# Encoder trunk in seven-product blocks: the up parts' two groups staggered, and the first weight sums issued at other places

## The chip, the cores and the metric

One core of a Trainium2 chip runs the program. The metric is the device time of one execution in microseconds (us). Short names: PE is TensorE (matmuls; PEld its weight loads), DVE is VectorE, ACT is ScalarE, POOL is GpSimd, SP is SyncE, which here only issues transfers.

## The reference

One layer of an encoder on 512 tokens of 1024 channels. The end of the layer is what matters here:

```python
x = x + token_mixer(rmsnorm(x, norm_mix), ...)
x = x + cross_attention(rmsnorm(x, norm_xattn), rmsnorm(mem, norm_mem), w_xq, w_xkv, w_xo)
x = x + squared_relu_mlp(rmsnorm(x, norm_mlp), w_up, w_down)
return rmsnorm(x, norm_final)

def squared_relu_mlp(xn, w_up, w_down):          # w_up 1024 x 4096, w_down 4096 x 1024
    return jnp.square(jax.nn.relu(xn @ w_up)) @ w_down
```

## The kernel before

The trunk function goes through the token mixer, the cross attention, and then three kinds of parts that this study is about: the **output part** (the attention's output times `w_xo`), and, four times, an **up part** and a **down part** of the MLP, each pair for 1024 of the 4096 hidden columns. The parts are numbered `st`: -1 is the output part, 0, 2, 4, 6 are up parts, 1, 3, 5, 7 down parts.

**Seven products.** Each part is a product of matrices that are cut in two by two blocks and multiplied with seven block products instead of eight. They are called P1 to P7. Each is done for two **groups** `g` (0 and 1, written a and b, so 3a is P3 of the first group); a group is half of the columns (up) or half of the inner dimension (down). A part so has 14 **jobs** (P, g). Every fp32 operand is split into a high and a low part (`split_out`, L258: ACT copies the high part, DVE subtracts it from the source), and a product is three matmuls (high x high, high x low, low x high). A job of an up part is 24 matmuls of 256 columns (L1471 to L1473), a job of a down part 12 of 512 columns (`product`, L1214 to L1216).

**Order of the jobs.** PE runs in the order that the program writes (`manual_schedule`). On ACT, DVE, POOL and SP the framework orders the instructions: of those that are ready, it takes the one that stands first in the program; what is inside `tc.high_priority()` comes before the rest. `MORDER` (L1127) lists the jobs of up parts (entry 0: 1a 2a 1b 2b 5a 5b 3a 3b 6a 6b 7a 7b 4a 4b) and of down parts (entry 1: 1a 1b 5a 5b 2a 2b 6a 6b 3a 3b 7a 7b 4a 4b, with 4a and 4b run together). `JOBS` (L1076) is the order of the output part: P1 P7 P2 P5 P6 P3 P4, each a then b.

**Weights.** P1, P2 and P3 take a block of the weights as it is; SP loads it into one of three `st` buffers (`mload`). The other four take sums of blocks, which POOL's transfers form: a first transfer writes a block into a buffer, further ones add blocks to it in the memory (`mfill` with `accumulate`, L1142). Two sums run per group. The *chain* begins as block (0,1) plus (0,0), which P5 uses; after P5's split (1,1) is added for P6, after P6's split (1,0) for P4. The *pair* is (0,1) plus (1,1), for P7. There are two buffers, `msum`: the one that holds the chain of a part holds the pair of the part before (`pair_buf` is `chain_buf(st + 1)`). So the next part's chain can begin when this part's P7 is split, and the next part's pair when this part's P4 is split. `sum_start(st, pair)` (L1150) issues the first two transfers of both groups; `msplit` (L1165) calls it after the splits of 7b and 4b, and splits the weights of each job into `wh` and `wl`. There are three buffers of each, so the split of a job begins when the job two places ahead of it begins (`mahead`, L1185).

For the first up part `sum_start` is called for chain and pair at job 8 of the output part (L1232), with all its transfers tied behind the last add of `w_xo` (`behind`, L1157). POOL also computes the power -1/2 of the norm, once for each half of the tokens (`rstd_half`, L1351); PE spreads the result over the partitions (`norm_half`, L1369), and from there come the MLP's activations `xf`.

**Banks and activations.** In an up part P1, P6, P7 and P4 of a group add up in one PSUM bank, P5 and P3 in a second one, and P2 has a third. Between two of them the bank is read: ACT copies P1 (L1477), P5 (L1484) and P6 (L1487), DVE subtracts P7 from a kept copy (L1492) and P2 adds with L1479. After the square of the ReLU (L1446, L1447) the results are combined into the seven **forms** that the down part takes as its left operand; `form` splits each into high and low. The forms for P1, P2 and P4 are made as soon as their product is read. Those for P5 (L1499), P3 and P6 (L1502, L1503) and P7 (L1507) need P4's result and are made, for both groups, after the last job of the up part. In a down part (`by_blocks`) P1, P6, P7 and P4 share two banks, P5 and P3 two, P2 has two; each finished product is added to the residual `xr` by DVE (`add_to`, L1418), and the next user of the bank waits for that.

## Time and profile before

| what | value |
|---|---|
| median of 3 runs | 871.79 us (869.49 to 872.32) |
| the profiled execution's own time | 872.12 us |
| its span, first to last instruction | 870.3 us |
| mean granted PE clock | 0.972 |
| busy: PE, DVE, ACT, POOL | 823.4, 624.8, 482.5, 116.8 us |
| transfers in the span | 131.53 MB, mean 151 GB/s |
| first up part to last down part | 508.35 to 863.0 us |

Durations that are quoted later come from the one profiled execution, so sums are made against its own time; it lies 1.8 us above its span and 0.3 us above the median of the runs.

How to read the rows: a timeline row has start and length in us, the engine, the line, the operation, what it writes and reads, its shape, how many instructions were merged, and in brackets the idle time of the engine just ahead of it with what ended it. A group row ends in the busy time, the mean length of one in ns, and the idle time ahead. A waits row has the total, how often, and the longest. A window row has the stretch, its length, the busy time and count of the engine that was asked for, the granted PE clock as a share of the full one, the busy share of the 16 DMA engines and their GB/s. A row of the chain that ended last has start, length and what it was.

### The profile page before, as it was taken

What the parts mean: (1) busy time and instruction counts of PE and PEld (TensorE: products, weight loads), DVE (VectorE), ACT (ScalarE), POOL (GpSimd) and SP (SyncE); (2) the same over time, 40 slices, a digit from 0 to 9 for tenths busy, and PEclk for the clock granted to TensorE, in tenths of its full rate; (3) what the DMA queues carried; (4) which work ended last, traced back from release to release, by engine and by line L of the source; (5) the groups of instructions that cost most, each with busy time, mean ns of one, the idle gap of its engine ahead of it and who ended that gap; (6) DMA issues with size and microseconds to landing.
All of it is one profiled execution on the core that took longest, in us unless ns stands there. A gap on an engine that the chain in (4) does not pass through costs nothing.

```text
span 870.3 us, 13082 instructions
## 1 busy us (share of the span) xinstructions
PE 823.4 (95%) x4990; PEld 708.7 (81%) x4990; DVE 624.8 (72%) x1033; ACT 482.5 (55%) x850; POOL 116.8 (13%) x164
## 2 busy tenths in 40 slices
PE   9999999999999999999999689979997999799976
PEld 6788888888889888878888579968996899589955
DVE  6568875898589896555679469966596659655876
ACT  5247455435685674554466457834683468336834
POOL 2000000000100001000001212203221322032301
PEclk9999999999999999999999979989998999799989
DMA  7332223132333345423523948979997999789962
GB/s 275 100 128 97 74 73 121 61 99 73 121 98 122 103 141 169 116 79 102 140 61 86 260 102 169 239 174 231 226 236 178 238 223 227 178 213 233 241 142 96
DMA packets 44752, 131.53 MB, mean 151 GB/s; under 512 B 4305, under 2 KB 4433, under 8 KB 44690
## 3 DMA queue, kind: packets, MB, share of 16 engines
q0 software_dynamic: 19648, 56.63, 31.7%
q1 hardware_dynamic: 24752, 73.60, 24.8%
q8 instruction: 39, 0.64, 0.3%
q10 hardware_dynamic: 290, 0.47, 0.2%
q14 instruction: 23, 0.19, 0.1%
HBM read 128.58 MB, written 2.10 MB: 150 GB/s over the span
## 4 chain that ended last, share of the span: by engine, by line
PE 61%; issue 14%; DMA 12%; DVE 6%; ACT 5%; POOL 2%; POOLq 0%; ACTq 0%; DVEq 0%
DMA as<-in_wpk 10%; PE mm L261 10%; PE mm L263 10%; PE mm L262 10%; PE sm L1214 4%; PE sm L1215 3%; PE sm L1216 3%; ACT wh L258 3%; PE mm L1472 3%; DVE wl L258 3%; PE mm L1473 3%; PE mm L1471 3%; PE sm L485 2%; PE sm L1471 2%; PE sm L1472 2%
## 5 line engine op out<-in xcount | busy, mean ns | idle before, releaser
L258 ACT ACTIVATE wh<-st 128x1024 fp32r<-128x1024 f32 x123 | 129.9, 1058 | 155.1 <-PE mm L262 43.7
L258 DVE TENSOR_TENSOR wl<-st,wh 128x1024 fp32r<-128x1024 f32 x123 | 150.2, 1223 | 83.1 <-ACT wh L258 82.2
L1142 POOL DMA_DIRECT2D as<-in_wpk x96 | 87.0, 968 | 261.4 <-DVE wl L258 166.8
L258 DVE TENSOR_TENSOR wl<-as,wh 128x1024 fp32r<-128x1024 f32 x66 | 80.8, 1224 | 52.3 <-ACT wh L258 52.0
L261 PE MATMUL mm<-xT,wh 128*128 128x512 f32 x288 | 115.4, 402 | 0.0
L263 PE MATMUL mm<-xT,wl 128*128 128x512 f32 x288 | 113.4, 394 | 0.1
L262 PE MATMUL mm<-xT,wh 128*128 128x512 f32 x288 | 112.7, 391 | 0.3 <-DVE xT L975 0.3
L258 ACT ACTIVATE wh<-as 128x1024 fp32r<-128x1024 f32 x66 | 69.7, 1056 | 77.2 <-DMA as<-in_wpk 25.1
L1214 PE MATMUL sm<-wh,a 128*128 128x512 f32 x180 | 75.1, 417 | 22.2 <-DVE vv L1418 22.2
L1216 PE MATMUL sm<-wh,a 128*128 128x512 f32 x180 | 73.7, 409 | 0.7 <-DVE a L258 0.7
L1215 PE MATMUL sm<-wl,a 128*128 128x512 f32 x180 | 73.7, 409 | 0.0
L263 PEld LDWEIGHTS mm<-xT,wl 128*128 128x128 f32 x288 | 54.1, 188 | 11.7 <-DVE wl L258 0.3
L261 PEld LDWEIGHTS mm<-xT,wh 128*128 128x128 f32 x288 | 54.2, 188 | 11.1 <-ACT wh L258 0.3
L262 PEld LDWEIGHTS mm<-xT,wh 128*128 128x128 f32 x288 | 54.2, 188 | 11.0 <-DVE xT L975 0.9
L1214 PEld LDWEIGHTS sm<-wh,a 128*128 128x128 f32 x180 | 36.2, 201 | 33.0 <-issue 20.8
L1216 PEld LDWEIGHTS sm<-wh,a 128*128 128x128 f32 x180 | 36.0, 200 | 9.1 <-DVE a L258 1.0
L1215 PEld LDWEIGHTS sm<-wl,a 128*128 128x128 f32 x180 | 36.3, 201 | 7.6
L1472 PE MATMUL sm<-xT,wh 128*128 128x256 f32 x128 | 36.7, 286 | 1.0 <-DVE xT L258 1.0
L1471 PE MATMUL sm<-xT,wh 128*128 128x256 f32 x128 | 36.9, 288 | 0.6 <-ACT xT L258 0.6
L199 POOL TENSOR_TENSOR tiny<-tiny,misc 128x4 f32<-128x4 f32 (+1 forms) x10 | 9.6, 965 | 204.6 <-DVE tiny L197 139.5
L1473 PE MATMUL sm<-xT,wl 128*128 128x256 f32 x128 | 36.6, 286 | 0.0
L1471 PE MATMUL mm<-xT,wh 128*128 128x256 f32 x128 | 36.3, 284 | 0.0
(387 smaller groups left out, 2135.5 us busy)
## 6 DMA issues: line engine op xcount, KB each, us to landing
st<-in_wpk SPq DMA_DIRECT2D x123, 512.0 KB, 3.7
as<-in_wpk POOLq DMA_DIRECT2D x100, 512.0 KB, 7.5
gate<-in_wpk POOLq DMA_DIRECT2D x8, 512.0 KB, 5.8
as<-in_x SPq DMA_DIRECT2D x4, 512.0 KB, 6.7
vv<-in_x SPq DMA_DIRECT2D x8, 256.0 KB, 4.1
out<-vv SPq DMA_DIRECT2D x7, 256.0 KB, 2.2
a<-in_mem SPq DMA_DIRECT2D x2, 512.0 KB, 3.7
t<-in_rows SPq DMA_DIRECT2D x2, 256.0 KB, 4.9
```

Of the source, the lines that this page charges most:

```text
L258: return sc.activation(dst_hi, src, AF.Copy), v.tensor_tensor(out=dst_lo, in0=src, in1=dst_hi.bitcast(F32), op=ALU.subtract)
L261: pe.matmul(ps, lhsT=ah, rhs=bh, start=first, stop=False)
L262: pe.matmul(ps, lhsT=ah, rhs=bl, start=False, stop=False)
L263: pe.matmul(ps, lhsT=al, rhs=bh, start=False, stop=last)
L485: mm = pe.matmul(ps[64 * i:64 * i + 64, z:z + 64], lhsT=kc[j][:, w * P + 64 * i:w * P + 64 * i + 64], rhs=rhs(j, w * P, i), start=True, st ...
L1142: return eng.dma_start(out=dst, in_=mblock(st, g, *b), **kw)
L1214: pe.matmul(ps, lhsT=ah, rhs=bh, start=new, stop=False, **fl)
L1215: pe.matmul(ps, lhsT=ah, rhs=bl, start=False, stop=False, **fl)
L1216: pe.matmul(ps, lhsT=al, rhs=bh, start=False, stop=end and k == 1, **fl)
L1471: pe.matmul(o, lhsT=hi[:, z], rhs=xh[:, m], start=new, stop=False, **fl)
L1472: pe.matmul(o, lhsT=hi[:, z], rhs=xl[:, m], start=False, stop=False, **fl)
L1473: pe.matmul(o, lhsT=lo[:, z], rhs=xh[:, m], start=False, stop=kt == 3, **fl)
```

## The change

Up parts get orders of jobs of their own. The first one: 1a 2a 1b 2b 5a 5b 3a 6a 3b 7a 6b 4a 7b 4b. The other three: 1a 2a 5a 3a 5b 1b 6a 2b 7a 6b 4a 3b 7b 4b. Down parts keep theirs. `sum_start` takes the groups that it is for, and `msplit` now calls it for each group by itself, after that group's P7 and P4.

The four late forms are made per group: those of the first group inside the up part, right after job 4a; of the second group the P5 form after 4b, and the P6, P3 and P7 forms by a function `ready`, which the down part calls ahead of its jobs 5a, 2a and 6a.

For the first up part the chain sums are issued at job 5 of the output part, tied to nothing; the pair sums are issued in `rstd_half` of the second half, tied behind its power.

```diff
             if p == "P6":
-                last_xo[0] = add_block(s_, block(-1, g, 1, 0))
+                add_block(s_, block(-1, g, 1, 0))
...
-    MORDER = ([("P1", 0), ("P2", 0), ("P1", 1), ("P2", 1)] + two("P5", "P3", "P6", "P7", "P4"), two("P1", "P5", "P2", "P6", "P3", "P7", "P4"))
-    MJ = [(st, p, g) for st in range(8) for p, g in MORDER[st % 2]]
+    seq = lambda s: [("P" + w[0], "ab".index(w[1])) for w in s.split()]
+    MORDER = [seq("1a 2a 1b 2b 5a 5b 3a 6a 3b 7a 6b 4a 7b 4b")] + [two("P1", "P5", "P2", "P6", "P3", "P7", "P4"),
+              seq("1a 2a 5a 3a 5b 1b 6a 2b 7a 6b 4a 3b 7b 4b")] * 4
+    MJ = [(st, p, g) for st in range(8) for p, g in MORDER[st]]
...
-    def sum_start(st, pair):
+    def sum_start(st, pair, gs, after=None):
...
-                for g in range(2):
+                for g in gs:
                     o = mfill(gp, (pair_buf if pair else chain_buf)(st, g), st, g, b, i > 0)
-                    if st == 0:
-                        behind(o, last_xo[0])
+                    if after is not None:
+                        behind(o, after)
...
-            if g == 1 and p in ("P7", "P4"):
-                sum_start(st + 1, p == "P4")
+            if p in ("P7", "P4"):
+                sum_start(st + 1, p == "P4", (g,))
...
-            if n == 8:
+            if n == 5:
                 msum.extend([A16(), A16()])
-                sum_start(0, False)
-                sum_start(0, True)
+                sum_start(0, False, (0, 1))
...
         for a in adds:
             behind(a, pw)
+        if u == 1:
+            sum_start(0, True, (0, 1), pw)
...
+        def first(g):
+            v.tensor_tensor(out=y[3, g], in0=y[2, g], in1=y[3, g], op=ALU.subtract)
+            form("P5", g, y[3, g], A4)
+
+        def second(g):
+            v.tensor_tensor(out=y[3, g], in0=y[3, g], in1=y[0, g], op=ALU.subtract)
+            form("P6", g, y[3, g], A4)
+
+        def third(g):
+            v.tensor_tensor(out=y[1, g], in0=y[1, g], in1=y[3, g], op=ALU.add)
+            form("P3", g, y[1, g], A4)
+
+        def fourth(g):
+            v.tensor_tensor(out=y[0, g], in0=y[0, g], in1=y[2, g], op=ALU.subtract)
+            form("P7", g, y[0, g], A4)
...
             elif p == "P4":
                 y[2, g] = T2()[:, 0:512]
                 square(y[2, g], ps)
-        for g in range(2):
-            v.tensor_tensor(out=y[3, g], in0=y[2, g], in1=y[3, g], op=ALU.subtract)
-            form("P5", g, y[3, g], A4)
-        for g in range(2):
-            v.tensor_tensor(out=y[3, g], in0=y[3, g], in1=y[0, g], op=ALU.subtract)
-            v.tensor_tensor(out=y[1, g], in0=y[1, g], in1=y[3, g], op=ALU.add)
-            form("P3", g, y[1, g], A4)
-        for g in range(2):
-            form("P6", g, y[3, g], A4)
-            v.tensor_tensor(out=y[0, g], in0=y[0, g], in1=y[2, g], op=ALU.subtract)
-            form("P7", g, y[0, g], A4)
+                first(g)
+                if g == 0:
+                    second(g)
+                    third(g)
+                    fourth(g)
...
+        def ready(p, g):
+            for at, fn in ((("P5", 0), second), (("P2", 0), third), (("P6", 0), fourth)):
+                if (p, g) == at:
+                    fn(1)
+                    hand(1)
...
-        by_blocks(2 * f + 1, sta, (sm2, mm2, sm2), lambda t, c, ps, sign, last: add_to(t, c, ps, sign, f == 3 and last))
+        by_blocks(2 * f + 1, sta, (sm2, mm2, sm2), lambda t, c, ps, sign, last: add_to(t, c, ps, sign, f == 3 and last), ready)
```

In the new text the P2 form of a group is made when both its P3 and its P6 are done; `hand` gives the down part the forms that exist so far.

## Prediction

> **What bounds the kernel now.** I read the page first, then the busy time by stretches, cut where TensorE's lines change from up products (L1471 to L1473) to down products (L1214 to L1216), then TensorE's waits, then the timelines around the two places that they name.

> ```profile
> PE 823.4 (95%) x4990; PEld 708.7 (81%) x4990; DVE 624.8 (72%) x1033; ACT 482.5 (55%) x850; POOL 116.8 (13%) x164
> 508.35:554.64 46.29, 43.25 (x345) 0.96 0.71 163
> 554.64:601.36 46.72, 41.57 (x171) 0.93 0.83 196
> 601.36:641.67 40.31, 40.31 (x337) 1.00 0.99 240
> 641.67:688.05 46.38, 41.19 (x171) 0.93 0.84 201
> 688.05:728.36 40.31, 40.31 (x338) 1.00 0.99 237
> 728.36:776.41 48.05, 41.57 (x170) 0.89 0.80 195
> 776.41:816.73 40.32, 40.32 (x338) 1.00 1.00 238
> 816.73:863.00 46.27, 40.17 (x170) 0.93 0.60 149
> PE sm L1214 <- DVE vv L1418: 22.2, 7, 6.1
> PE sm L1369 <- POOL tiny L1351: 9.9, 1, 9.9
> ```

> TensorE (PE) is busy for 95%, so only its holes are to be had. The eight stretches are up and down in turn; the columns are length, PE busy, granted clock, DMA share and GB/s. The last three up parts take 40.31 us without a hole and at clock 1.00: 14 jobs of 2.88 us. The down parts take 46.27 to 48.05 us and lose clock. The waits say where: 22.2 us in the down parts, and 9.9 us once, ahead of L1369.

> That one first: POOL's timeline ahead of it, PE's row, and the clock in that stretch.

> ```profile
> 477.50 2.51 POOL L1142 DMA_DIRECT2D as<-in_wpk  x3
> 500.41 1.18 POOL L1142 DMA_DIRECT2D as<-in_wpk  x1 [8.22 <-DMA as<-in_wpk]
> 501.16 1.17 POOL L1351 TENSOR_TENSOR tiny<-tiny,misc 128x2 f32<-128x2 f32 x1
> 502.38 0.69 PE L1369 MATMUL sm<-cs,tiny 128*128 128x128 f32 x2 [9.88 <-POOL tiny L1351]
> 497.74:507.98 10.24, 5.60 (x14) 0.50 0.65 122
> ```

> The power that the first half's norm needs (L1351) stands on POOL behind the eight transfers of the first up sums; the last accumulate waits 8.22 us for the transfer it adds to. PE stands for 9.88 us, and the clock falls to 0.50.

> Now the first down part: the DMA on the chain of waits, then ACT, DVE and PE; below them the first matmuls of jobs 1 and 5.

> ```profile
> 560.69 11.54 DMA as<-in_wpk
> 568.77 1.06 ACT L258 ACTIVATE wh<-as 128x1024 fp32r<-128x1024 f32 x1 [4.67 <-DMA as<-in_wpk]
> 566.80 0.67 DVE L1418 TENSOR_TENSOR vv<-vv,sm 128x512 f32<-128x512 f32 x1
> 569.87 1.23 DVE L258 TENSOR_TENSOR wl<-as,wh 128x1024 fp32r<-128x1024 f32 x1 [2.39 <-ACT wh L258]
> 576.90 1.87 DVE L1418 TENSOR_TENSOR vv<-vv,sm 128x512 f32<-128x512 f32 x3
> 577.64 0.80 PE L1214 MATMUL sm<-wh,a 128*128 128x512 f32 x1 [4.08 <-DVE vv L1418]
> 576.25:583.07 6.82, 5.43 (x13) 0.50 0.69 154
> 554.64 0.40 PE L1214 MATMUL sm<-wh,yT 128*128 128x512 f32 x1
> 565.55 0.39 PE L1214 MATMUL mm<-wh,gate 128*128 128x512 f32 x1
> 647.46 11.78 DMA as<-in_wpk
> 735.75 11.45 DMA as<-in_wpk
> 822.82 12.74 DMA as<-in_wpk
> ```

> Four jobs take 10.91 us, 2.73 each, so a down part without holes is 14 x 2.73 = 38.2 us. P6 adds to the banks of P1, so PE has to wait until DVE has read P1 out (L1418). One such read runs at 566.80; the next stand behind the split of P6's weights, which waits for a sum that lands 11.54 us after its issue, and behind forms of the activations. They run at 576.90, though P1 was over by 560. PE loses 4.08 us, and 6.8 us at half clock. The last three rows are the same transfer on the chain in the other down parts. So a down part is bounded by late sums and by DVE's order, not by the amount of work.

> **The change part by part.** *First sums.* The chain sums move to job 5 of the output part, whose P5 weights free the buffer; the pair sums move behind the second power.

> ```profile
> 514.19 0.70 POOL L1351 TENSOR_TENSOR tiny<-tiny,misc 128x2 f32<-128x2 f32 x1 [11.87 <-DVE tiny L1349]
> DMA to landing us min/median/max: 3.2/7.3/12.7
> 508.35:555.00 46.65, 41.45 (x50) 0.96 0.71 165
> 531.63 0.39 PE L1472 MATMUL mm<-yT,wh 128*128 128x256 f32 x1 [1.00 <-DVE yT L258]
> ```

> The first power then finds POOL free, and the 9.88 us go. At half clock 5.60 us of matmuls cost 2.8 us more than at full, so at most 12.7 us are gained. But DVE, busy for 41.45 of the 46.65 us that follow, is late next: PE already waits 1.00 us for P3's activations at 531.63. I take 11.0; the ends are 8.9 (one more wait of 1.0) and 12.7. The chain sums pass the two adds of P6 on POOL and share the DMA engines with SP's loads; they go out three jobs of 2.73, some 8 us, before today's 477.50, so two medians of 7.3 us in a row end by 485, ahead of the power, which is ready when PE goes idle at 492.5. [...] The new wait: the pair sums stand behind the second power, about 503 instead of 514.19. Two chained medians bring them to 518; P7 of the first group is job 9, due near 529 (554.64 less 11.0 and five jobs of 2.88) and split two jobs earlier at 523. Nothing, with 5 us to spare; beyond that each us late is a us on PE. Behind the power stand only the P5 adds.

> *Down parts.* Today both groups' P7 and P4 follow each other, so the next part's sums bunch. POOL's sum transfers by stretches (busy, count, clock, DMA share, GB/s):

> ```profile
> 521.00:540.00 19.00, 4.76 (x4) 1.00 0.72 141
> 540.00:562.00 22.00, 7.39 (x10) 1.00 0.99 250
> ```

> Ten are issued in 22 us at DMA share 0.99, four in the 19 us before. With the groups staggered, P7 and P4 of the first group split as jobs 8 and 10 instead of 10 and 12, so that group's four transfers go two jobs (5.8 us) earlier and are done as the down part begins. In front of P5's adds then stands one pair accumulate instead of two. I estimate that the adds land about 3 us sooner after their issue: 8.5 instead of 11.54. The second add today lands at 572.2; P6's second group would be due at 554.64 + 7 x 2.73 = 573.8 and its split takes 2.3 us, so it was late by only about a us. Also, the second group's P6, P3 and P7 forms are now put out inside the down part, after P1's reads in the program, so these reads no longer queue behind them. What is late next is the read of P7's bank before P4, for which I leave 0.4 us a part. The four parts take 187.4 us; 4 x 38.6 is 154.4: 33.0 saved. The ends are 34.6 (nothing left) and 0 (below). A loss I exclude for the DMA side: the transfers are the same in number and start no later, but for the second group's chain sums, one job later and needed only at job 3. SP's loads spread out from the first four jobs to jobs 0, 1, 3, 5: nothing.

> *Up parts: two waits that the change adds.* In the last three up parts 3a follows 5a at once and adds to the bank that ACT must first copy; in all four 4b follows 7b at once, on a bank that DVE must first subtract. Today a job lies between them. Timelines of ACT and DVE, and groups of DVE:

> ```profile
> 615.83 1.06 ACT L258 ACTIVATE wh<-st 128x1024 fp32r<-128x1024 f32 x1
> 616.80 0.58 ACT L1484 ACTIVATE t<-mm 128x512 f32<-128x512 f32 x1
> 636.11 0.69 DVE L1492 TENSOR_TENSOR t<-t,sm 128x512 f32<-128x512 f32 x1 [0.43 <-PE sm L1473]
> L258 DVE TENSOR_TENSOR a<-t,a 128x512 fp32r<-128x512 f32 x24 | 16.5, 686 | 1.4 <-ACT a L258 1.4
> L1502 DVE TENSOR_TENSOR t<-t,as 128x512 f32<-128x512 f32 x8 | 5.5, 684 | 0.0
> L258 DVE TENSOR_TENSOR wl<-as,wh 128x1024 fp32r<-128x1024 f32 x64 | 78.4, 1224 | 52.0 <-ACT wh L258 51.7
> ```

> For 3a: at the end of 5a ACT starts a weight split at 615.83, and the copy is over at 617.38, so PE waits 1.6 us (0.8 if the copy goes first, 2.6 with a second split ahead). While 3a waits, the following jobs' split has gone on; nothing else queues on PE but the later jobs. For 4b: the subtract takes 0.69 us and can begin with the end of 7b: 1.0 us at best. But four forms of the first group stand ahead of it in the program, eight DVE pieces of 0.69, or 5.5 us. They can begin about 2.1 us after 4a, behind a split and two squares on ACT; of the 5.8 us until the end of 7b some 3.7 are left, and two splits of 1.22 and a subtract of 0.68 take 3.1 of these. If all that goes first, with one more piece for P2's form, the subtract ends 5.9 us after 7b. The row at 636.11 speaks for the short end, the reads that waited until 576.90 behind program-earlier forms for the long one; between rows of equal weight I take the middle, 3.4 us. In the first up part 7b follows 4a directly, so the forms aren't ready yet: 1.3 us (1.0 to 2.0).

> *The sum,* against the profiled execution, 872.12 us with a span of 870.3: -11.0 + 1.3 + 3 x (1.6 + 3.4) - 33.0 = -27.7, so a span of 842.6 and a time of 844.4. The median of the runs shown, 871.79, is 0.3 below that execution: 844.

> [...] The idle stretches that here went with half clock were 4.08 us and more, and the 1.00 us one did not. [...] The trace has no idle stretch between the two sizes. [...]

> **The rivals.** *The new wait at 4b is the long one.* All forms of the first group go ahead of the subtract: 5.9 us instead of 3.4, long enough for the half clock, which in 576.25:583.07 cost half of 5.43, 2.7 us. 3 x (2.5 + 2.7) = 15.6 more: 860. For it speaks that the order on DVE follows the program among what is ready; against it that DVE has holes while it waits for ACT (52.0 us in the row of the splits).
> *The down parts keep their holes.* The adds of P5 still wait in POOL's line behind a pair accumulate and the DMA engines, 0.99 busy in the up parts, stay full. It decides where the second add takes over some 10.6 us to land instead of 11.54. Then the 33.0 us aren't saved while the new waits stay: 877, slower by 5. Against it: the DMA share falls to 0.83 in the down part, and one accumulate less is ahead.
> *The change doesn't free the power.* Nothing ties the chain accumulates to a place ahead of the first power but their earlier readiness; if they wait there again, 9.9 us come back: 854.

> **How the numbers follow.** The forecast 844 has 0.54, the long wait 0.32, the holes that stay 0.06, the power that stays behind 0.08. The low end takes the good ends: -12.7 + 1.0 + 3 x (0.8 + 1.0) - 34.6 = -40.9, which is 831. The high end is the first rival with 1.0 more at each 3a: 863. That leaves out the second rival and the tails. About 0.3%, 2.6 us, is what a measurement of this kernel can tell from no change. All but the second rival are faster by more: 0.92; slower 0.06; the rest, where the ends of two cases cancel, 0.02.

> **What would show it.** Right: no wait of L1369 on POOL beyond a us or two; down parts of 38 to 39 us at clock 1.00; the waits of L1214 on L1418 under 2 us in all; up parts of 45 us with a wait of L1471 on ACT L1484 near 1.6 and on DVE L1492 near 3.4. Wrong: up parts near 50 us with half clock at their end (first rival), down parts still over 45 us with a DMA of 11 us on the chain (second), or the 9.9 us still ahead of L1369 (third).

## The result: slower by 0.8%

| | median | ratio to before, 95% interval |
|---|---|---|
| before | 871.79 us (869.49 to 874.07, 7 runs) | |
| after | 878.85 us (875.74 to 882.65, 7 runs) | 1.0082 [1.0055, 1.011] |

The forecast was 844 us with a range of 831 to 863. The profiled execution of the changed kernel took 878.85 us with a span of 877.1. Of the four executions of `e12_no_handout`, one of the kernels below, one took 2069.5 us against 863.94 to 866.19 for the others, and no time below counts it.

This is the same cut by parts as before, TensorE alone (length, busy time and matmul rows, granted clock, DMA share, GB/s); the first row is the first up part.

```profile
496.09:549.10 53.01, 47.08 (x345) 0.90 0.74 183
549.10:599.04 49.94, 41.75 (x170) 0.90 0.78 182
599.04:650.14 51.10, 42.92 (x337) 0.93 0.94 232
650.14:688.91 38.77, 38.39 (x171) 1.00 0.81 183
688.91:741.36 52.45, 43.32 (x338) 0.91 0.94 232
741.36:780.48 39.12, 38.74 (x170) 0.99 0.76 174
780.48:831.28 50.80, 42.72 (x337) 0.93 0.95 232
831.28:869.74 38.46, 38.46 (x170) 1.00 0.52 121
```

| part | before | after | change | forecast of the change |
|---|---|---|---|---|
| start of the first up part | 508.35 | 496.09 | -12.3 | -11.0 |
| first up part | 46.29 | 53.01 | +6.7 | +1.3 |
| first down part | 46.72 | 49.94 | +3.2 | -8.1 |
| three later up parts | 120.94 | 154.35 | +33.4 | +15.0 |
| three later down parts | 140.70 | 116.35 | -24.4 | -24.9 |

The first and the last row came as forecast, within 1.3 us. Three went wrong, all to the long side: the later up parts by 18.4 us, the first down part by 11.3, the first up part by 5.4. TensorE's waits (total, how often, the longest) name three places:

```profile
PE sm L1490 <- ACT a L258: 20.3, 3, 7.1
PE mm L1490 <- ACT t L1503: 6.8, 4, 2.1
PE sm L1216 <- ACT a L258: 6.8, 1, 6.8
PE sm L1216 <- DVE vv L1421: 1.1, 3, 0.4
```

The first row is 4b in the later up parts, the second 3a in all four, the third 5b in the first down part. The last row was 22.2 us before the change.

**The power.** POOL's timeline shows the power (now L1352) run as soon as its input is there; its matmul (now L1372) follows on TensorE at 492.69 without a wait:

```profile
491.92 0.71 POOL L1352 TENSOR_TENSOR tiny<-tiny,misc 128x2 f32<-128x2 f32 x1 [13.82 <-DVE tiny L1350]
```

**4b.** VectorE's queue around the end of 7b in the second up part (the dots stand for rows left out), then TensorE's row for 4b. 7b ended 6.67 us ahead of 645.07, at 638.40.

```profile
636.43 0.69 DVE L1458 TENSOR_TENSOR t<-t,t 128x512 f32<-128x512 f32 x1
637.04 0.68 DVE L1509 TENSOR_TENSOR rg<-mm,rg 128x512 f32<-128x512 f32 x1
637.64 1.21 DVE L258 TENSOR_TENSOR wl<-st,wh 128x1024 fp32r<-128x1024 f32 x1
638.77 0.68 DVE L258 TENSOR_TENSOR a<-t,a 128x512 fp32r<-128x512 f32 x1
639.49 0.69 DVE L1462 TENSOR_TENSOR t<-t,as 128x512 f32<-128x512 f32 x1
...
643.64 0.68 DVE L1470 TENSOR_TENSOR as<-as,t 128x512 f32<-128x512 f32 x1
644.24 0.68 DVE L1513 TENSOR_TENSOR t<-t,sm 128x512 f32<-128x512 f32 x1
645.07 0.55 PE L1490 MATMUL sm<-xT,wh 128*128 128x256 f32 x1 [6.67 <-ACT a L258]
```

The stretch of half clock around it, all engines (PE, PEld, DVE, ACT, POOL, then clock and transfers):

```profile
643.06:649.89 6.83, 4.82 (x22) 4.85 (x23) 3.24 (x6) 2.49 (x4) 1.30 (x2) 0.50 0.92 232
```

VectorE has no hole in this stretch. L1458, L1462, L1466 and L1470 and the low halves behind them are the four forms of the first group; 7b's subtract (L1513), which 4b waits for, comes last. The row names ScalarE as the releaser, but that form is of the first group and only happened to end at 644.99; the subtract, which 4b needs, ended at 644.92, 0.15 us ahead of 4b. In the stretch of half clock 4.82 us of matmuls ran at 0.50, which costs 2.4. So this part is 40.31 + 1.52 at 3a + 6.67 at 4b + 2.4 = 50.9, measured 51.10.

**5b in the first down part.** The timelines of ScalarE, VectorE and TensorE:

```profile
551.80 0.63 ACT L1450 ACTIVATE t<-t 128x512 f32<-128x512 f32 x1
558.24 1.06 ACT L258 ACTIVATE wh<-as 128x1024 fp32r<-128x1024 f32 x1 [5.81 <-DMA as<-in_wpk]
563.53 0.63 ACT L258 ACTIVATE a<-t 128x512 fp32r<-128x512 f32 x1 [1.30 <-DVE t L1458]
559.33 1.23 DVE L258 TENSOR_TENSOR wl<-as,wh 128x1024 fp32r<-128x1024 f32 x1 [5.92 <-ACT wh L258]
562.81 0.68 DVE L1458 TENSOR_TENSOR t<-t,t 128x512 f32<-128x512 f32 x1
564.21 0.79 PE L1216 MATMUL sm<-wh,a 128*128 128x512 f32 x1 [6.76 <-ACT a L258]
```

And the transfer on the chain of work that ended last:

```profile
546.60 11.56 DMA as<-in_wpk
```

The second group's sum for 5b is issued at 546.60 and lands 11.56 us later. The split of those weights heads the queues of ScalarE and VectorE meanwhile, and the square of 4b was over at 552.4; yet L1458, the first step of 5b's form, runs at 562.81, behind the split. So the late sum cost more than its own lateness; `e12b_no_handout` below shows how much more.

**3a in the first up part.** There 5b lies between 5a and 3a, and the forecast had no wait. ScalarE and TensorE:

```profile
520.05 1.06 ACT L258 ACTIVATE wh<-as 128x1024 fp32r<-128x1024 f32 x1 [4.24 <-DMA as<-in_wpk]
...
521.96 0.58 ACT L1503 ACTIVATE t<-mm 128x512 f32<-128x512 f32 x1
522.59 0.38 PE L1490 MATMUL mm<-yT,wh 128*128 128x256 f32 x1 [2.05 <-ACT t L1503]
```

The new order has 6a right behind 3a, so the split of 6a's weights comes up two jobs ahead of that, while its sum is still under way; the copy of 5a's result stands behind it on ScalarE. Right behind the wait, 523.60 to 527.01 ran at half clock, with TensorE busy throughout, which costs another 1.7 us.

### The profile page after: what moved, and what is told of

Its sections match the earlier page's. It is cut to its first block, busy times and chain, and to the rows that moved or that the text cites. A ratio compares the mean times of both kernels' runs of the same rounds, so it can differ in the third digit from the quotient of the medians.

```text
span 877.1 us, 13066 instructions
## 1 busy us (share of the span) xinstructions
PE 824.6 (94%) x4990; PEld 711.7 (81%) x4990; DVE 624.6 (71%) x1033; ACT 484.2 (55%) x850; POOL 117.1 (13%) x164
## 4 chain that ended last, share of the span: by engine, by line
PE 57%; DMA 14%; issue 10%; DVE 9%; ACT 6%; POOL 2%; POOLq 0%; ACTq 0%; DVEq 0%
DMA as<-in_wpk 12%; PE mm L261 11%; PE mm L263 11%; PE mm L262 10%; DVE wl L258 3%; PE sm L1218 3%; PE sm L1216 3%; PE sm L1217 3%; ACT wh L258 3%; PE sm L485 2%; POOL as L1144 2%; DMA gate<-in_wpk 2%; PE sm L827 1%; PE mm L1216 1%; PE mm L1218 1%
## 5 line engine op out<-in xcount | busy, mean ns | idle before, releaser
L258 DVE TENSOR_TENSOR wl<-st,wh 128x1024 fp32r<-128x1024 f32 x123 | 150.1, 1222 | 71.5 <-ACT wh L258 70.8
L258 ACT ACTIVATE wh<-st 128x1024 fp32r<-128x1024 f32 x123 | 129.6, 1057 | 127.8 <-PE mm L262 43.7
L258 DVE TENSOR_TENSOR wl<-as,wh 128x1024 fp32r<-128x1024 f32 x66 | 80.8, 1224 | 76.2 <-ACT wh L258 75.3
L258 ACT ACTIVATE wh<-as 128x1024 fp32r<-128x1024 f32 x66 | 69.9, 1059 | 106.7 <-DMA as<-in_wpk 29.9
L1216 PE MATMUL sm<-wh,a 128*128 128x512 f32 x180 | 71.6, 398 | 7.9 <-ACT a L258 6.8
L1218 PE MATMUL sm<-wh,a 128*128 128x512 f32 x180 | 71.2, 396 | 1.1 <-DVE a L258 1.1
L1217 PE MATMUL sm<-wl,a 128*128 128x512 f32 x180 | 71.0, 395 | 0.0
L1490 PE MATMUL sm<-xT,wh 128*128 128x256 f32 x128 | 40.8, 319 | 21.8 <-ACT a L258 20.3
L1216 PEld LDWEIGHTS sm<-wh,a 128*128 128x128 f32 x180 | 34.3, 191 | 16.7 <-ACT a L258 7.2
L1490 PEld LDWEIGHTS sm<-xT,wh 128*128 128x128 f32 x128 | 28.3, 221 | 23.0 <-ACT a L258 20.9
L1491 PE MATMUL sm<-xT,wh 128*128 128x256 f32 x128 | 40.1, 314 | 1.7 <-DVE xT L258 1.7
L1218 PEld LDWEIGHTS sm<-wh,a 128*128 128x128 f32 x180 | 34.3, 191 | 9.0 <-DVE a L258 1.8
L1217 PEld LDWEIGHTS sm<-wl,a 128*128 128x128 f32 x180 | 34.4, 191 | 7.1
L1492 PE MATMUL sm<-xT,wl 128*128 128x256 f32 x128 | 39.8, 311 | 0.0
```

The costliest lines, as they stand in the source:

```text
L258: return sc.activation(dst_hi, src, AF.Copy), v.tensor_tensor(out=dst_lo, in0=src, in1=dst_hi.bitcast(F32), op=ALU.subtract)
L1216: pe.matmul(ps, lhsT=ah, rhs=bh, start=new, stop=False, **fl)
L1217: pe.matmul(ps, lhsT=ah, rhs=bl, start=False, stop=False, **fl)
L1218: pe.matmul(ps, lhsT=al, rhs=bh, start=False, stop=end and k == 1, **fl)
L1490: pe.matmul(o, lhsT=hi[:, z], rhs=xh[:, m], start=new, stop=False, **fl)
L1491: pe.matmul(o, lhsT=hi[:, z], rhs=xl[:, m], start=False, stop=False, **fl)
```

## The experiments

The theory: each of the three losses is one instruction that stands in its engine's queue behind something that need not go first. The main rival: the stagger, or the waits of 4b and 5b, cost that much whatever the order on ScalarE and VectorE. Ratios are to the kernel before in the same series (medians there 872.4 to 875.1 us). "Sums" is the moved first sums, "handing out" the forms made between the down products.

| kernel | sums | handing out | stagger | median | ratio, 95% interval |
|---|---|---|---|---|---|
| e5_sums_only | yes | | | 860.48 | 0.9871 [0.9822, 0.9919] |
| e3_handout_only | | yes | | 861.37 | 0.9866 [0.9828, 0.9905] |
| e2_orders_back | yes | yes | | 848.00 | 0.9709 [0.967, 0.9749] |
| e12_no_handout | yes | | yes | 865.93 | 0.989 [0.9867, 0.9913] |
| after | yes | yes | yes | 878.85 | 1.0082 [1.0055, 1.011] |

### One instruction moved: the subtract behind 7b

```diff
-                v.tensor_tensor(out=y[3, g], in0=y[3, g], in1=ps, op=ALU.subtract)
+                with tc.high_priority():
+                    v.tensor_tensor(out=y[3, g], in0=y[3, g], in1=ps, op=ALU.subtract)
```

> The changed kernel with one instruction moved in VectorE's queue: the subtract behind 7b is written with high priority, so that it stands behind the second form's subtract and ahead of five of the first group's other pieces. Jobs, orders, sums and forms are as changed. Theory (4b waits for the subtract, and the subtract for its place in VectorE's queue): 4b's wait in the last three up parts falls from 6.6 to 7.1 us to 2.5 to 3.5 us, each such part from 51 us to about 47 us, or 44 us where the half clock at its end goes too; time 862 to 869 us. Rival (4b waits for its weights or for ScalarE, the subtract's place only goes along with that): the gap and the time stay, 876 to 881 us.

868.19 us, ratio 0.9954 [0.9927, 0.9981]. VectorE and TensorE at the same place (L1514 is the subtract), and the cut of the second up part:

```profile
637.22 0.69 DVE L1462 TENSOR_TENSOR t<-t,as 128x512 f32<-128x512 f32 x1
637.83 0.68 DVE L1514 TENSOR_TENSOR t<-t,sm 128x512 f32<-128x512 f32 x1
638.66 0.36 PE L1490 MATMUL sm<-xT,wh 128*128 128x256 f32 x1 [2.27 <-DVE t L1514]
```

```profile
597.02:641.61 44.59, 40.80 (x338) 1.00 0.94 238
```

The subtract now stands behind L1462, and 4b waits 2.27, 2.98 and 2.69 us in the three parts; they take 44.59, 48.60 and 46.49 us. The rival falls: the place in VectorE's queue alone was worth about 4 us a part, and more where the half clock went with it.

### The three pieces of the change apart

e2 puts back the orders, e3 puts the sums back too:

```diff
-    MORDER = [seq("1a 2a 1b 2b 5a 5b 3a 6a 3b 7a 6b 4a 7b 4b")] + [two("P1", "P5", "P2", "P6", "P3", "P7", "P4"),
-              seq("1a 2a 5a 3a 5b 1b 6a 2b 7a 6b 4a 3b 7b 4b")] * 4
+    MORDER = [[("P1", 0), ("P2", 0), ("P1", 1), ("P2", 1)] + two("P5", "P3", "P6", "P7", "P4"),
+              two("P1", "P5", "P2", "P6", "P3", "P7", "P4")] * 4
```

> The changed kernel with both orders of the up parts put back (the two groups side by side); the forms are still handed out between the down products and the first sums issued in mid-output. Theory (the stagger alone costs the last three up parts their 10.5 to 12.1 us; the handing out alone gives the down parts their 7.6 to 8.9 us): last three up parts 40.3 us each, last three down parts 38.5 to 39.5 us, the output part 12 us shorter, the first up part 47 to 50 us; about 832 us, and up to 845 us if the first down part still waits at 5b. Rival (the down parts became short because the staggered up part finishes the first group early, so the handing out needs the stagger): down parts 44 to 46 us, 855 to 862 us.

> The handing out of the forms alone: orders of the up parts and places of the first sums as before the change. Theory (the three parts of the change add up): the four down parts 38.5 to 40 us instead of 46 to 48 us, all else as before, 840 to 846 us. Rival (the handing out needs the stagger): 866 to 873 us.

> The kernel before with the first weight sums alone issued at the changed kernel's places; orders and forms as before. Theory (the freed power shortens the output part by 12 us, and the first up part gives 2 to 4 us of it back at its start, where its first products wait for the normalised input): first up part starts at 496 us and takes 48 to 50 us instead of 46.3 us; time 861 to 864 us. Rival (the 5.4 us that the first up part lost beyond the forecast all come from the moved sums, which land later for it): first up part 52 to 53 us, time 866 to 868 us.

e5 came in just below its range (860.48), and its first up part, 48.50 us, is the theory's. e2's cut, the second up part and the second down part:

```profile
589.75:630.81 41.06, 40.81 (x337) 1.00 1.00 232
630.81:672.47 41.66, 38.93 (x170) 1.00 0.91 223
```

TensorE at 5b of the second down part:

```profile
642.24 0.50 PE L1218 MATMUL sm<-wh,a 128*128 128x512 f32 x1 [2.16 <-DVE a L258]
```

The up parts are short again, 40.3 to 41.1 us, as the theory has it. The down parts are not 38.5 to 39.5 us but 41.7, 41.9 and 44.8, since 5b now waits 2.16 us for the low half of its form (4b, which the form needs, is the job just ahead of the down part). In the last one 5b waits 1.03 us more and half clock comes in. So e2 missed its 832 us by 16 (by 3 the 845 us that it gave for a wait at 5b in the first down part, which was 2.52 us), and e3 its 840 to 846 us by 15; neither came into its rival's range. What I took for the handing out's gain in the later down parts was the stagger's in part. The sums and the handing out do add up: 12.1 and 11.2 us below 872.53, together 24.5.

The fourth corner is the stagger without handing out: the late forms are all written behind the up part.

```diff
                 square(y[2, g], ps)
-                first(g)
-                if g == 0:
-                    second(g)
-                    third(g)
-                    fourth(g)
+        for fn in (first, second, third, fourth):
+            for g in range(2):
+                fn(g)
```

> The changed kernel, staggered and with its sums in mid-output, but with no form handed out: all the groups' last forms are written behind the up part again. Theory (stagger and handing out conflict: the forms handed out stand ahead of 7b's subtract in VectorE's queue): 4b waits at most 3 us in the last three up parts, which take 42 to 45 us instead of 51 us; the down parts get part of their holes back, 41 to 46 us instead of 38.8 us; 865 to 877 us. Rival (the stagger makes 4b late by itself, whatever stands in the queue): up parts stay at 50 to 52 us and the down parts grow, over 885 us.

Its 865.93 us are in the theory's range. A second run of the same kernel gave the trace:

> The staggered kernel without the handing out once more, for its trace. It was timed at 865.9 us where the changed kernel has 878.9 us. Theory (stagger and handing out conflict in VectorE's queue): the last three up parts 42 to 45 us, 4b waiting at most 3 us, and the down parts 41 to 46 us. Rival (the gain over the changed kernel lies in the first up and down parts, and 4b still waits 6 us and more later on): the last three up parts 48 us or more, with the first up and down parts together under 95 us.

865.22 us, span 863.4. The second pair of parts, then TensorE at 4b in it:

```profile
593.64:641.29 47.65, 42.54 (x338) 0.96 0.92 234
641.29:680.30 39.01, 38.59 (x170) 1.00 0.84 193
```

```profile
636.85 0.36 PE L1490 MATMUL sm<-xT,wh 128*128 128x256 f32 x1 [3.12 <-DVE t L1513]
```

Here both expectations missed in part. 4b waits 3.12 to 3.22 us, just over the theory's 3, and the up parts are 47.6 to 48.5 us, 3 above it. But the down parts, 39.0 to 40.2 us, are about as short as after the change, 38.5 to 39.1: with the first group finished early, what it has ready fills VectorE's holes without being handed out (in the second up part its first form, L1458, runs at 632.10, ahead of 7b's subtract at 636.02).

This trace also parts the two costs at 5b in the first down part. VectorE and ScalarE there:

```profile
551.74 0.68 DVE L1458 TENSOR_TENSOR t<-t,t 128x512 f32<-128x512 f32 x1
557.71 1.06 ACT L258 ACTIVATE wh<-as 128x1024 fp32r<-128x1024 f32 x1 [6.46 <-DMA as<-in_wpk]
```

The sum is nearly as late as after the change (the split starts at 557.71 instead of 558.24), but L1458 of the second group stands ahead of the split, and 5b waits 2.11 us instead of 6.76. So some 2 us are the sum's lateness, and the other 4.6 the form's place behind the split, where the handing out had put it.

By lengths, in us:

| | sums only | + handing out | + stagger | all three |
|---|---|---|---|---|
| first up and down part | 96.94 | 93.75 | 97.35 | 102.95 |
| three later up parts | 120.93 | 122.49 | 143.74 | 154.35 |
| three later down parts | 143.24 | 128.34 | 118.61 | 116.35 |

The stagger alone gives 24.6 us in the later down parts and takes 22.8 in the up parts: a wash. The handing out on top of it adds 10.6 us to the up parts and 5.6 to the first pair, and takes 2.3 off the later down parts. Without the stagger it is worth 16.5 us by these lengths. They are of single executions, and the one of "sums only" took 866.17 us, 5.7 above that kernel's median; by the medians the handing out is worth 12.5 us there. The ratios say the same: the stagger takes 0.987 to 0.989, within the noise, the handing out 0.987 to 0.971 without the stagger and 0.989 to 1.008 with it. Both pieces shorten the later down parts, and each is in the other's way.

### The first down part: where 7b stands

```diff
-    MORDER = [seq("1a 2a 1b 2b 5a 5b 3a 6a 3b 7a 6b 4a 7b 4b")] + ...
+    MORDER = [seq("1a 2a 1b 2b 5a 5b 3a 6a 3b 7a 6b 7b 4a 4b")] + ...
```

> The changed kernel with 7b one place earlier in the first up part (6b 7b 4a 4b at its end instead of 6b 4a 7b 4b); nothing else. Theory (the first down part's 5b stood 6.8 us because the second group's weight sum is sent only after 7b's weights are split and behind the first group's pair sum, and the form of 5b is queued behind that split): 5b's wait 2 to 4 us, the first down part 45 to 47 us instead of 49.9 us, time 873 to 876 us. Rival (5b waits for its form, which is late because the up part ends on 4b; the sum is not what ends last): wait 6 to 7 us and time 877 to 880 us.

872.10 us, ratio 1.0006 [0.9983, 1.0029]. The first pair's cut, and the only wait left at 5b:

```profile
495.79:552.25 56.46, 45.14 (x345) 0.94 0.75 179
552.25:592.66 40.41, 38.97 (x171) 1.00 0.89 215
```

```profile
562.40 0.50 PE L1218 MATMUL sm<-wh,a 128*128 128x512 f32 x1 [1.02 <-DVE a L258]
```

The down part falls by 9.5 us, more than expected. The split of 5b's weights now starts at 555.20 without a wait for its sum, and 5b's form is no longer held up behind it. The up part is 3.4 us longer, since 7b now waits 2.31 us for the copy of 6b's result and 3a waits 5.75 us (the same split of 6a's weights, with a sum that landed later in this execution).

The same was then seen with the sign turned. e13 takes the order of the first up part for the last three and the old one for the first, with the subtract moved up; e14 does so with the order of e8, the subtract where it was.

> The kernel with the up parts' orders put back (e2_orders_back), but the last three up parts in the order that the change gave the first one (staggered at its end only: 3a 6a 3b 7a 6b 4a 7b 4b), and the subtract moved up in VectorE's queue. Theory (a milder stagger keeps what the down parts gained, 2.8 to 6.3 us each, and costs less than that in the up part): up parts 41.5 to 43 us, down parts 38.5 to 40 us, 840 to 845 us. Rival (every stagger pays more at 4b than it brings): up parts 44 us or more, 850 to 858 us.

> As e13_end_only, but ending 7a 6b 7b 4a 4b and with the subtract where it was written: 4a lies between 7b and 4b and covers the subtract, while 7b comes straight behind 6b and waits for the copy of 6b's result. Theory (the cover takes the wait at 4b away, and 7b waits 2.3 us as in the run e8_seq0_7b): up parts 42 to 43.5 us, down parts 39 to 42 us, 843 to 849 us. Rival (the wait at 4b does not depend on the distance to 7b): up parts 45 us or more, over 850 us.

e13 took 866.17 us, 0.9902 [0.9877, 0.9927], and e14 853.51 us, 0.9753 [0.9728, 0.9778]. e13, the second pair, with the waits at 4b and 5b:

```profile
587.93:630.47 42.54, 40.81 (x337) 1.00 0.93 233
630.47:678.58 48.11, 42.32 (x171) 0.89 0.81 189
```

```profile
627.50 0.38 PE L1490 MATMUL sm<-xT,wh 128*128 128x256 f32 x1 [0.78 <-DVE t L1514]
643.18 0.80 PE L1216 MATMUL sm<-wh,a 128*128 128x512 f32 x1 [4.36 <-ACT a L258]
```

Neither side of e13's expectation holds: 4b is cured (0.78 us each, up parts 42.2 to 42.5), yet the down parts get the late 5b, 46.4 to 48.1 us. In e14, with 7b one place earlier, that wait is 1.02 us and the down parts are 40.4, 40.4 and 43.0 us; its up parts are 43.9 to 45.0, as 7b waits 1.9 us and 3a 1.2 to 2.3. That is 4.5 us above its theory's range, although the wait at 4b is gone as the theory had it. In both kernels 4b is the last job; 7b's place is what differs at 5b. (The subtract is moved up in e13 alone, but in e7, where it is the only change, 5b waits 5.08 us all the same.)

### Cures put together

e9 is e7 with 5b between 5a and 3a. e11 is e9 with the order of e8 in the first up part and P2 ahead of P5 in the down parts. e10 and e15 start from e2: e10 has P2 ahead of P5 in the down parts, e15 makes 5b's form first.

> The kernel with the subtract moved up in VectorE's queue (the run e7_sub_prio) and besides 5b put between 5a and 3a in the last three up parts. Theory (3a waits only for the copy of 5a's result, and a product between them covers it): the wait of 1.5 to 1.75 us at 3a goes in three parts, 4 to 5 us off e7_sub_prio: 861 to 865 us. Rival (ScalarE's queue is what is late, and the wait shows up at the next product that needs it): 866 to 869 us.

> The changed kernel with every cure at once and the stagger kept: the subtract moved up in VectorE's queue, 5b between 5a and 3a, 7b earlier in the first up part, P2 before P5 in the down parts. Theory (the stagger itself buys nothing: each of its last three up parts still ends with 4b waiting 2 to 3 us for the subtract, and its down parts are no shorter than those of e10_back_p2): 842 to 852 us, 6 to 14 us behind e10_back_p2. Rival (with its waits cured the stagger pays, since the first group is finished early): within 2 us of e10_back_p2 or ahead of it.

> The kernel with the up parts' orders put back (the run e2_orders_back) and besides P2 before P5 in the down parts, its forms handed out in that order. Theory (what is left in the down parts is 5b waiting for the second group's first form, which is made after 4b; two more products in front of it cover that): down parts 38.5 to 40 us instead of 41.7 to 45.6 us, 10 to 14 us off e2_orders_back: 833 to 839 us. Rival (VectorE and ScalarE are full over the seam, and the wait only moves to a later product): 845 to 849 us.

> The kernel with the up parts' orders put back (e2_orders_back), with the second group's first form written with high priority and the first group's other three forms written behind it. Theory (what is left in those down parts is 5b waiting 2.2 to 3.5 us for that form, which stands behind three forms of the first group in VectorE's queue): the wait at 5b is under 0.7 us, down parts 39 to 41 us instead of 41.7 to 45.6 us, 837 to 842 us. Rival (VectorE is full over the seam, so what is put back there is late instead): the waits move to other products, 846 to 850 us.

| kernel | median | ratio, 95% interval | what moved |
|---|---|---|---|
| e9_prio_5b | 865.85 | 0.9932 [0.9909, 0.9955] | 3a's wait gone; up parts 3.7 us shorter than e7's, down parts 3.5 longer |
| e11_stagger_all | 863.72 | 0.991 [0.9879, 0.9941] | 17 us behind e10; up parts 47.0 to 49.6, down parts 38.7 to 40.4 |
| e10_back_p2 | 846.77 | 0.9718 [0.9688, 0.9748] | down parts 42.1 to 43.6 |
| e15_back_first_prio | 851.43 | 0.9737 [0.9715, 0.9759] | 5b's wait gone; 6a stands instead |

The theories of e9, e10 and e15 took the wait away and not the time, or little of it: e9 is 2.3 us below e7, between its theory and its rival, and the two intervals overlap. In e15, 5b no longer waits, but three jobs later 6a waits for its weights, here in the second pair's down part, whose length is 45.01 where e2 has 41.66:

```profile
646.73 0.65 PE L1216 MATMUL sm<-wh,a 128*128 128x512 f32 x1 [2.28 <-ACT wh L258]
```

The rivals of e10 and e15 hold (e15 came out 1.4 us above its rival's range): VectorE is full over the seam (in e2 it has no idle stretch over 0.3 us from 542.2 to 558.0, across the first one), and what is put ahead there makes another thing late. With all its cures the stagger stays 17 us behind e10, where the theory of e11 gave 6 to 14, and the theory's reason holds only in part. 4b still waits 1.43 to 2.97 us, as it said. But the last three down parts are 9.5 us shorter in all than e10's, not level with them; the up parts lose 22.8 us, more than that, since in two of them 6a also waits, 3.22 and 2.56 us, for a weight split whose sum is late. e2 and e10 are the best of this study, level with each other, 2.8 to 2.9% faster than before; e15's interval overlaps theirs.

## Why the prediction was wrong

**First sums: right, under 1 us short.** The power was freed and the first up part starts 12.3 us earlier, where 11.0 stood for the net gain. What comes late next is more than the "one more wait of 1.0": with the sums alone (e5) the first up part starts 12.45 us earlier and is 2.21 us longer, so 10.2 stay. For the two adds of P6, which the chain sums pass on POOL, the forecast counts no loss. No run shows how long a first transfer of these sums alone would hold them up; after the change both wait for a weight split (0.75 us ahead of 473.92, 2.47 us ahead of 477.26), not for a sum.

**3a: right in the later parts.** 1.6 us stood, 1.52, 1.75 and 1.52 came. Wrong in the first up part, for which the prediction had no wait at 3a: the order changes not only the products but the splits, and with 6a moved up, its split waits for a sum with the copy behind it. The kernels with that first order (after, e7, e9, e12b) show a wait of 1.45 to 3.84 us there, e11 and e8, where 6a stands at the same place, 2.56 and 5.75; e2, e5, e13, e14 and e15, with the old order, show none on that copy, and e10, also with the old order, 1.71 us one job later, at 3b, behind the same split. No run moves the copy alone, so the cause is read from the traces.

**4b: the step that failed.** The prediction listed what could stand ahead of the subtract, came to 1.0 us if nothing did and 5.9 if all did, and then: "between rows of equal weight I take the middle, 3.4 us". The case was not between two rows. The working gave the forms of the first group a start of 3.7 us ahead of the end of 7b (the trace has 2.0: 636.43 against 638.40), and they come first in the program. After the change all four are begun ahead of the subtract (L1470 at 643.64, the subtract at 644.24), and 4b waits 6.56 to 7.12 us. e7 shows that it was their place: one instruction moved, 2.27 to 2.98 us. The wait brought half clock besides, which the middle value had left out: 2.2 to 3.0 us a part. This is the first rival, which priced a part at 40.31 + 1.6 + 5.9 + 2.7 = 50.5 us; 50.80 to 52.45 came. All three waits of 6.56 us and more had the half clock; shorter ones went both ways: one of 1.75 us brought it in e8, and one of 3.21 us did not in e12b (last section).

**Down parts: the size right in three, the reason half right, the first one wrong.** 38.6 stood and 38.46 to 39.12 came, where the prediction credited earlier sums, and reads that no longer queue behind forms handed out. e12b has 39.0 to 40.2 us without any handing out; e2, with it and without the stagger, 41.7 to 44.8. So the stagger does most of it; in the staggered kernel the handing out adds only 2.3 us to that gain, and its price at 4b, 10.6 us over the three up parts, was put too low. For the first down part the failed step is the exclusion: the second group's chain sums go "one job later and needed only at job 3". In the first up part 7b comes straight behind 4a, so the two groups' transfers bunch; the accumulate took 11.56 us, and the split that waits for it holds up ScalarE and VectorE with the form of 5b behind it: 6.76 us at 5b and 10.24 us of half clock around it, where nothing stood. e8 undoes that with one job moved (40.41 us instead of 49.94), e13 brings it to parts that did not have it, and in e12b, with the sum as late but the form ahead of the split, 5b waits 2.11 us.

**The sum and the range.** The 34.5 us between the forecast 844.4 and 878.85 are 18.4 in the later up parts (first rival), 11.3 in the first down part and 5.4 in the first up part (no case of the prediction; mostly 3a's 2.05 us and the 1.7 us of half clock behind it), less 1.3 at the power; the later down parts and the end add 0.7. The first rival alone would have made 860, inside the range. The range broke because each new order was costed at the waits of TensorE's banks, and not at what the same order does to the splits and sums. That the second rival's 877 is close is chance: its holes were in the first down part alone.

## What to carry to other kernels

When a change reorders products, list for each engine's queue what the new order puts ahead of what, and follow the last wait from there. Here ScalarE's copy stood behind a split that waited 4.24 us for its sum, VectorE's form behind one that waited 5.92 us, and, before the change, POOL's power behind an accumulate that waited 8.22 us. A value between two ends is no answer where the program sets the order: with one instruction moved, 4b's wait in the second up part was 2.27 us instead of 6.67. Work handed to an engine "early" can stand ahead of what the bottleneck waits for, as the first group's forms did ahead of the subtract: give the instruction that the bottleneck waits for the first place, and see who is behind an instruction that waits for a transfer. Test two cures for the same hole one by one: here, on top of the moved sums, one gains alone and the other breaks even, and together they lose.

## What the runs showed of the hardware

```profile
807.95:811.36 3.41, 0.72 (x6) 1.00 1.02 329
811.36:814.77 3.41, 3.41 (x18) 0.50 0.96 264
```

In the last up part of e12b, 4b waited longer, 3.21 us, until 812.88, and the whole part has clock 1.00. Two steps shared that wait, and each was busy for over half:

```profile
807.83:811.25 3.42, 1.84 (x16) 1.00 1.01 205
811.25:814.66 3.41, 1.78 (x15) 1.00 0.97 380
```

The fourteen traces, cut into these steps from 490 us to the end of the last down part, bear it out. Of the steps at full clock, 51 had TensorE busy for under 0.45 of their length, and all 51 were followed by half clock; 1278 had it busy for over 0.57, and none was; of the 31 between, 10 were. A step at half clock was the last one where its busy share was 0.85 or more, and was followed by another where it was less; of the closest two, the one from 511.39 before the change was busy for 2.92 us and was the last, and the one from 499.70 after it for 2.90 us and was not. The traces of before and after alone have 11 steps under 0.45, all followed by half clock, 177 over 0.57, none of them, and 3 between, of which 1.

So the length of a wait set no border here. One of 1.75 us at 3a in e8 did (half clock from 693.18), and the same 1.75 us at that place after the change did not; the step was busy for 1.66 us both times, inside the undecided band. In the kernel before, several short ones did, the longest of them 0.57 and 0.96 us, at the start of the first up part, in a step in which TensorE was busy for 1.88 us (507.98 to 511.39):

```profile
511.39:514.81 3.42, 2.92 (x14) 0.50 0.53 162
```

The prediction overlooked this stretch where it says "The idle stretches that here went with half clock were 4.08 us and more". The price of one step is some 1.7 us where TensorE is busy throughout: half of 3.41 us, as from 523.60 to 527.01 after the change.
